# Attention values computed up front for all heads, token-major, as two units of seven products, in a hybrid attention and mLSTM kernel

## The chip, the cores and the metric

The kernel runs on one core of one Trainium2 chip. The metric is the time of one execution on the device in microseconds (us), as the median of several runs: 1439.41 us before (three runs, 1439.31 to 1439.99). Beside the times there is one profiled execution, whose span is 1437.5 us.

The core has a tensor engine (PE in the rows, TensorE in the text; PEld is its weight load), a vector engine (DVE, VectorE), a scalar engine (ACT, ScalarE), GpSimd (POOL) and SyncE (SP), which does nothing here but issue DMAs. Each engine works through its own instructions in the order in which they stand in the program, and engines wait for each other by semaphores.

## The reference

A model of two layers (h + mixer, then h + gated feed-forward, each behind a norm; a final norm) on 512 tokens of 1024 channels, in float32. The first layer's mixer is the dilated attention that the change touches (`xn` below is the normalised input), the second's an mLSTM.

```python
SEQ, D_MODEL, DEPTH = 512, 1024, 2
DIL_CONFIGS = ((128, 1), (512, 4), (2048, 16))     # window, dilation of the three groups
ATTN_HEADS, ATTN_HEAD_DIM = 8, 128
...
def dilated_attention_mixer(xn, positions, w_in, w_out):
    B, S, _ = xn.shape
    proj = (xn @ w_in).reshape(B, S, N_GROUPS, 3, ATTN_HEADS, ATTN_HEAD_DIM)
    scale = ATTN_HEAD_DIM ** -0.5
    outs = []
    lses = []
    for g, (window, dilation) in enumerate(DIL_CONFIGS):
        q = apply_partial_rope(proj[:, :, g, 0], positions) * scale
        k = apply_partial_rope(proj[:, :, g, 1], positions)
        v = proj[:, :, g, 2]
        o, lse = dilated_window_attention(q, k, v, window, dilation)
        outs.append(o)
        lses.append(lse)
    wts = jax.nn.softmax(jnp.stack(lses), axis=0)
    o = jnp.einsum('gbsh,gbshd->bshd', wts.astype(xn.dtype), jnp.stack(outs))
    return o.reshape(B, S, ATTN_WIDTH) @ w_out
```

In the attention, the projection of the normalised tokens gives queries, keys and values for three groups (g0, g1, g2: dilations 1, 4, 16) and eight heads of 128 columns. Each group's attention has its own softmax, and the groups are joined by a softmax over their log-sums. With 512 tokens g1 and g2 are four independent residues of 128 tokens each, and g0 is a band of blocks.

## The kernel before, in words

**Precision.** A float32 product is made of three fp32r matmuls, high x high, high x low and low x high (SPLITS). Every operand is therefore split in two: ScalarE copies it to fp32r (the high part, `_h`), VectorE subtracts that from the original (the low part, `_l`). For weights this is `split_chunk` (L203 to L210): a chunk is 128 x 1024 floats, 512 KB, loaded by SP in `load_chunk` (L200), high part on ScalarE (L208), low part on VectorE (L209). Three raw chunks, three high and three low parts are in flight (W_BUFS). The activations x are transposed at the start and split into eight pairs of tiles, `xa_h` and `xa_l` (`split_act`, L223 to L227), of 128 channels x 512 tokens each; the tokens stand in the order residue by residue ("token-major by residue"), so that g1 and g2 find their 128 tokens together.

**The normaliser.** x is split without its reciprocal norm r, which is applied to results. r is made by VectorE in small steps (`inverse_rms`, L307): a Newton iteration, a split of r into `xrhl`, eight diagonals `xdg` (L323), and two matmuls `xbc` (L329) that spread r over all partitions; VectorE copies this to `xrbc` (L330). `xrbc` scales queries and keys; `rtok`, r per token as a column, scales the token-major values.

**Projections.** `project` (L244) makes 256 columns (two heads of one group) of queries or keys channel-major: weights stationary, 512 tokens moving, 48 matmuls of 128x512 in two weight chunks (k0 and k1) of 24. VectorE reads out the result times `xrbc` (L724 for g0, L726 for the others), shuffles 32 partitions for the rotary embedding (L535), multiplies by the sines (L538) and adds (L541). `project_tokens_wide` (L281) makes the g1 and g2 values of a pair: 128 tokens stationary, 512 columns moving (256 of g1, 256 of g2), four chunks of 24 matmuls, rows L289 (loads) and L297 (matmuls); ScalarE copies the results with the scale r (L767).

**The attention, pair by pair.** Four pairs of heads, `a0` to `a3` (`attention_pair`, L552). For each: queries and keys of g0, g1, g2, then the values g0v (channel-major by `project`, into `vf`) and g12v. In between stand the softmax stages: `scores0` (L566, matmuls L575, masked maximum on VectorE L581, exponentials on ScalarE), `scores12` (L588, L595, L598), then `joint` (L640), which joins the groups after `exchange` (L622, a small matmul L631), `turn` (L668: eight TensorE transposes that make the g0 values token-major, in natural token order, with ScalarE copies out), `weigh` (L658) on VectorE, `transposes` (L677: 32x32 block transposes of the weights on VectorE, L681, then out to DRAM by POOL's queue, L684), `bring` (L687, back by one transfer each, L689), and `values` (L692, L699 and L704), the product with the values.

**What sets the order.** The code is written stage by stage, and `defer(n, fn)` puts a stage aside until n more weight chunks are through (`advance`, L142). RUN_AT gives these counts for scores0, scores12, the joint stage and the values, LAST_AT for scores12 and the joint stage of the last pair. So the softmax of a pair is laid between the projections of its values and of the next pair's queries and keys. `run` and `fenced` keep TensorE's order as written. SP's loads stand in the order in which chunks are asked for.

**The out-projection** takes eight heads (`oT`) split into high and low, weights `awo` in 256-column pieces c = 0 to 3. For the last pair (L804 to L813) the first weight chunk's products of c = 0 and 1 and parts of the second stand before and between that pair's two `values`.

**The start.** x arrives in four pieces; `first_mm` makes the first g0 query (`facc`) while x is still transposed; then the first g0 key (a0g0k), with `xbc` inside it; then g1's query and so on.

## Time and profile before

| | |
|---|---|
| median of three runs | 1439.41 us (1439.31 to 1439.99) |
| span of the profiled execution | 1437.5 us |
| TensorE busy | 1423.9 us (99%) |
| TensorE weight load busy | 1248.8 us (87%) |
| VectorE busy | 954.5 us (66%) |
| ScalarE busy | 605.4 us (42%) |
| GpSimd busy | 53.2 us (4%) |
| SP's and the other engines' hardware DMA queues | 131.55 MB, 29.6% of 16 DMA engines |
| DMA queue of POOL (software) | 16.30 MB, 3.7% |

The profiled execution's own time is its span of 1437.5 us, from its first to its last record; the runs, which are taken from outside, have a median 1.9 us above it. The rows of the profile give a start in us, a duration, an engine, a line (L239 is line 239 of the kernel whose profile it is), the operation, output<-inputs by the program's names, and a shape; x8 at the end: eight instructions in succession. A bracket at the end is the idle time of the engine before the row, and what released it. The 40 slices of the page each cover 36 us, and a digit is a busy share in tenths. Matmul rows start one after the other at less than their own length, since they are pipelined.

### The profile page before, as it was taken

The page shows a single profiled execution, that of the slowest core. Times are in us where ns is not written, and L with a number is a line of the kernel's source. Part 1 is how long each engine was busy: PE and PEld are TensorE (multiplying, and loading weights), DVE is VectorE, ACT ScalarE, POOL GpSimd, SP SyncE. Part 2 cuts the span into 40 slices and gives each one's busy share as a digit, 9 for nine tenths or more (in the row PEclk, how much of TensorE's full clock was granted, in tenths as well). Part 3 has the DMA queues.
Part 4 walks back from the last instruction along what each step waited for, and adds up shares of the span by engine and source line. Part 5 has one row for each costly group of instructions (what it writes and reads, how often), then busy time and mean ns, then how long its engine had stood idle before and what let it go on. Part 6 is the DMA issues. An engine that isn't in the chain of part 4 may idle for free. (4 is left out here: it accounts for less than half of the span.)

```text
span 1437.5 us, 20297 instructions
## 1 busy us (share of the span) xinstructions
PE 1423.9 (99%) x8050; PEld 1248.8 (87%) x8050; DVE 954.5 (66%) x1663; ACT 605.4 (42%) x1031; POOL 53.2 (4%) x91
## 2 busy tenths in 40 slices
PE   9999999999999999999999999999999999999998
PEld 7888888888888888999998888798888899998887
DVE  7857556557567487787782358987758777776233
ACT  5333224224225343544462233785434345455223
POOL 1001001001001000000000010100000000001001
PEclk9999999999999999999999999999999999999999
DMA  6326225234334424323233232222232333224231
GB/s 193 99 89 197 75 88 182 90 103 134 122 103 124 148 88 132 104 74 118 89 96 95 95 97 82 82 73 60 74 103 89 117 118 107 77 82 132 74 105 72
DMA packets 130903, 150.27 MB, mean 105 GB/s; under 512 B 6324, under 2 KB 120308, under 8 KB 130808
## 3 DMA queue, kind: packets, MB, share of 16 engines
q1 hardware_dynamic: 125616, 131.55, 29.6%
q0 software_dynamic: 3536, 16.30, 3.7%
q8 instruction: 63, 1.03, 0.3%
q10 hardware_dynamic: 1656, 1.12, 0.2%
q14 instruction: 32, 0.26, 0.1%
HBM read 138.99 MB, written 9.96 MB: 104 GB/s over the span
## 5 line engine op out<-in xcount | busy, mean ns | idle before, releaser
L1440 PE MATMUL fin<-fw_h,f1hh 128*128 128x512 f32 (+1 forms) x198 | 72.8, 368 | 0.0
L1440 PE MATMUL fin<-fw_l,f1hh 128*128 128x512 f32 (+1 forms) x198 | 72.6, 366 | 0.0
L1440 PE MATMUL fin<-fw_h,f1hl 128*128 128x512 f32 (+1 forms) x198 | 72.5, 366 | 0.0
L209 DVE TENSOR_TENSOR fw_l<-fw_w,fw_h 128x1024 fp32r<-128x1024 f32 x22 | 27.1, 1233 | 65.5 <-ACT fw_h L208 65.5
L239 PE MATMUL fo<-f0hh,fo_k_h 128*128 128x512 f32 x176 | 68.5, 389 | 0.0
L239 PE MATMUL fo<-f0hl,fo_k_h 128*128 128x512 f32 x176 | 68.5, 389 | 0.0
L239 PE MATMUL fo<-f0hh,fo_k_l 128*128 128x512 f32 x176 | 68.5, 389 | 0.0
L209 DVE TENSOR_TENSOR fo_k_l<-fo_k_w,fo_k_h 128x1024 fp32r<-128x1024 f32 (+1 forms) x24 | 27.2, 1134 | 62.0 <-ACT fo_k_h L208 62.0
L208 ACT ACTIVATE fo_k_h<-fo_k_w 128x1024 fp32r<-128x1024 f32 (+1 forms) x24 | 23.7, 989 | 74.7 <-PE fo L239 74.6
L208 ACT ACTIVATE fw_h<-fw_w 128x1024 fp32r<-128x1024 f32 x22 | 23.3, 1060 | 67.8 <-PE fin L1440 63.6
L1440 PEld LDWEIGHTS fin<-fw_l,f1hh 128*128 128x128 f32 x198 | 37.4, 189 | 6.0 <-DVE fw_l L209 0.2
L1440 PEld LDWEIGHTS fin<-fw_h,f1hh 128*128 128x128 f32 x198 | 37.4, 189 | 6.0
L1440 PEld LDWEIGHTS fin<-fw_h,f1hl 128*128 128x128 f32 x198 | 37.3, 189 | 6.0
L239 PEld LDWEIGHTS fo<-f0hh,fo_k_h 128*128 128x128 f32 x176 | 33.0, 188 | 6.9
L239 PEld LDWEIGHTS fo<-f0hl,fo_k_h 128*128 128x128 f32 x176 | 33.1, 188 | 6.9
L239 PEld LDWEIGHTS fo<-f0hh,fo_k_l 128*128 128x128 f32 x176 | 33.1, 188 | 6.7
L239 PE MATMUL f1j<-n_h,f1j_h 128*128 128x512 f32 x96 | 37.5, 391 | 0.0
L239 PE MATMUL f0j<-n_h,f0j_h 128*128 128x512 f32 x96 | 37.5, 391 | 0.0
L239 PE MATMUL f0j<-n_h,f0j_l 128*128 128x512 f32 x96 | 37.4, 390 | 0.0
L239 PE MATMUL f1j<-n_h,f1j_l 128*128 128x512 f32 x96 | 37.4, 390 | 0.0
L239 PE MATMUL f1j<-n_l,f1j_h 128*128 128x512 f32 x96 | 37.4, 389 | 0.0
L239 PE MATMUL f0j<-n_l,f0j_h 128*128 128x512 f32 x96 | 37.4, 389 | 0.0
(2101 smaller groups left out, 4859.7 us busy)
## 6 DMA issues: line engine op xcount, KB each, us to landing
f0j_w<-in_ffn_w_in_dram SPq DMA_DIRECT2D x28, 512.0 KB, 4.9
f1j_w<-in_ffn_w_in_dram SPq DMA_DIRECT2D x28, 512.0 KB, 3.6
fw_w<-in_ffn_w_out_dram SPq DMA_DIRECT2D x22, 512.0 KB, 3.9
fo_k_w<-in_ffn_w_out_dram SPq DMA_DIRECT2D x20, 512.0 KB, 3.5
awo_k_w<-in_attn_w_out_dram SPq DMA_DIRECT2D x8, 512.0 KB, 7.4
mv_k_w<-in_mlstm_w_in_dram SPq DMA_DIRECT2D x8, 512.0 KB, 3.6
mqk_k_w<-in_mlstm_w_in_dram SPq DMA_DIRECT2D x8, 512.0 KB, 3.7
mo_k_w<-in_mlstm_w_in_dram SPq DMA_DIRECT2D x8, 512.0 KB, 3.7
```

The lines of the kernel that those rows point to most:

```text
L208: nc.scalar.activation(hi[:, :n], raw[:, :n], AF.Copy)
L209: nc.vector.tensor_tensor(lo[:, :n], raw[:, :n], hi[:, :n].bitcast(F32), op=ALU.subtract)
L239: nc.tensor.matmul(acc, whl[a][:, k, m * P:(m + 1) * P], pairs[b][kk], start=(kk == 0 and (a, b) == SPLITS[0]), stop=(kk == nk - 1 and (a, ...
L1440: nc.tensor.matmul(acc[i][:, cs], a[a_][kk][:, tb * P:(tb + 1) * P], whl[b_][:, k, cs], start=(kk == 0 and (a_, b_) == SPLITS[0]), stop=(k ...
```

## The change

**Values.** All g0 values (1024 columns) and the g1 and g2 values of heads 0 to 3 (pairs 0 and 1; 512 columns each) are made (`values_stage`) right after the first g0 key, before the first g1 query. The g0 values form one unit `v0`, two halves of 512 columns; the g1 and g2 values of heads 0 to 3 form a second unit `v12`, whose two "halves" are g1's and g2's 512 columns. Pairs 2 and 3 make their g1 and g2 values as before. Each unit is a Strassen-Winograd scheme: the product of weights (1024 channels x 2 x 512 columns) with tokens (1024 channels x 2 x 256 tokens) as seven block products instead of eight (V_ORDER: a11, a12, s1, s2, s3, s4, a22), each of 24 matmuls with 128 tokens stationary and 512 weight columns moving, in two weight chunks of 12.

**Sums ahead.** The scheme needs sums of token blocks and of weight blocks. The tokens' forms T1 to T4 are made once, on VectorE, from a fresh copy of x times the gain (eight scalings L557, differences L561, L566, L567, L572), and split into high (ScalarE) and low (VectorE, L545 and L547); both units use them. The weight sums are made twice per unit, partly on VectorE (L637, L640), partly by loads of POOL's queue that add to what is in the tile (L604: a22 onto a21, later a21 onto a11); plain loads go by SP (L606). Results accumulate across products in PSUM (c, p, u banks), are copied out by ScalarE (L647), and two products are folded onto what was copied out, by VectorE (L650).

**Layout.** v0's results come out token-major by residue, into two staging tiles `vstage0` and `vstage1`. 32 copies of 64 KB on SP's queue (`settle`, L694) lay them out in natural order as `v0`, in the place ("heads") of the fresh copy of x. The head outputs later overwrite the g0 values head by head. `turn`, the 32 TensorE transposes and `natural_rstd` (with its small matmul) are gone. v12's results are used as they come, since g1 and g2 take tokens by residue.

**Order.** The values of pairs 0 and 1 no longer stand between the softmax stages; RUN_AT and LAST_AT are one chunk earlier for the later stages. In the out-projection three column pieces, c = 0, 1 and 2, instead of two have their first chunk ahead of the last pair's values. Some tiles of the start (angles, cosines, squares) move to other buffers.

The matmuls of the program go from 4220 to 4172 of the 128x512 form, and from 204 to 172 of the 128x128 form.

```diff
-RUN_AT = (2, 3, 5, 10)
-LAST_AT = (2, 4)
+RUN_AT = (2, 2, 4, 9)
+LAST_AT = (1, 3)
...
-        def natural_rstd():
...
-        defer(4, natural_rstd)
...
+            def scaled(ks):
+                for k in ks:
+                    nc.vector.tensor_scalar(xg[:, k], h[k], col("attn", k), None, op0=ALU.mult)
+
+            def first():
+                scaled(range(4))
+                nc.vector.tensor_tensor(z, half1(lo_), half2(lo_), op=ALU.subtract)
+                token_form("T1", z)
+
+            def second():
+                scaled(range(4, 8))
+                nc.vector.tensor_tensor(half2(lo_), half2(hi_), half2(lo_), op=ALU.subtract)
+                nc.vector.tensor_tensor(half2(hi_), half2(hi_), z, op=ALU.add)
+                token_form("T2", half2(hi_), -1.0)
+
+            def third():
+                token_form("T3", half2(lo_))
+                nc.vector.tensor_tensor(half1(hi_), half2(hi_), half1(hi_), op=ALU.subtract)
+                token_form("T4", half1(hi_))
...
+        V_ORDER = (("a11", "B11"), ("a12", "B21"), ("s1", "T1"), ("s2", "T2"), ("s3", "T3"), ("s4", "B22"), ("a22", "T4"))
+
+        class Values:
...
+            def prepare(self, n=1):
+                for _ in range(n):
+                    if not self.todo:
+                        return
+                    if not self.raw:
+                        self.begin()
+                    key, ch = self.todo.pop(0)
+                    first, own = self.raw["first", ch], self.raw["own", ch]
+                    nm = "%s%s%d" % (self.name, key, ch)
+                    if key in ("a12", "a22"):
+                        src = self.raw[key, ch] = wp.tile([P, 1024], F32, tag="wraw", name=nm + "_w", bufs=W_BUFS)
+                        self.load(key, ch, src)
+                    else:
+                        src = first if key in ("a11", "s3") else own
+                    self.made.append(split_chunk((src, 1024, lambda t: t.rearrange("p (k n) -> p k n", k=2), nm)))
+                    if key == "s1":
+                        nc.vector.tensor_tensor(own, own, first, op=ALU.add)
+                        self.load("a21", ch, first, True)
+                    elif key == "s2":
+                        nc.vector.tensor_tensor(own, own, self.raw["a12", ch], op=ALU.add)
+
+            def run(self, following, hooks={}):
...
+                    for ch in range(2):
+                        whl = self.made.pop(0)
+                        (self.prepare if self.todo else following)(1)
+                        for t in range(2):
+                            with fenced():
+                                for k in range(2):
+                                    for a, b in SPLITS:
+                                        nc.tensor.matmul(
+                                            banks[name][t], token_tile(okey, a, 2 * ch + k, t), whl[b][:, k],
+                                            start=(fresh and (ch, k) == (0, 0) and (a, b) == SPLITS[0]),
+                                            stop=((ch, k) == (1, 1) and (a, b) == SPLITS[-1]), skip_group_check=True)
...
+                        elif key == "a12":
+                            copy(dest(0, t), bk, r(t))
...
+                        elif key == "s3":
+                            fold(dest(1, 2 + t), bk, nr(2 + t))
...
+        def staged_values():
+            stage = [ap.tile([P, TB, 512], F32, tag="v12", name="vstage%d" % i, bufs=2) for i in range(2)]
+
+            def settle(i):
+                for c in range(4):
+                    for b in range(4):
+                        nc.sync.dma_start(v_all[0][32 * c:32 * c + 32, b, i * 512:(i + 1) * 512],
+                                          stage[i][32 * b:32 * b + 32, c])
+            return stage, settle
...
+        v0_unit = Values("v0", [columns(2 * D), columns(2 * D + 512)], lambda i, tb: stage[i][:, tb])
+        v12_unit = Values("v12", [columns(5 * D), columns(8 * D)], lambda i, tb: v_all[1][i][:, tb])
+        stage, settle = staged_values()
+        nrtok = ap.tile([P, TB], F32, name="nrtok")
+        nc.vector.tensor_scalar(nrtok, rtok, -1.0, None, op0=ALU.mult)
+        both(v0_unit.prepare)
+
+        def values_stage():
+            forms = token_forms()
+            v0_unit.prepare()
+            forms[0]()
+            v0_unit.run(v12_unit.prepare, {"a12": forms[1], "s1": forms[2]})
+            v_all.append(ap.tile([P, TB, D], F32, tag="heads", name="v0"))
+            for i in range(2):
+                settle(i)
+            vq = [ap.tile([P, TB, 512], F32, tag="v12", name="vq%d" % i, bufs=2) for i in range(2)]
+            v_all.append(vq[::-1])
+
+            def g1q(n):
+                ready.append(split_chunk(weight_chunk(w_in, len(ready), 3 * D, 4, "a0g1q_k%d" % len(ready))))
+            v12_unit.run(g1q)
...
-                (joint, turn, lambda: weigh(0), lambda: transposes(0), lambda: weigh(1), lambda: transposes(1),
+                (joint, lambda: weigh(0), lambda: transposes(0), lambda: weigh(1), lambda: transposes(1),
...
-            project(pair, w_in, 2 * D + pr * 256, KC, evac_f, nm + "g0v")
+            if pr < 2:
+                vt.extend(lambda c, i, g=g: v_all[1][g][:, c, (2 * pr + i) * P:(2 * pr + i + 1) * P] for g in range(2))
+                return values
...
         out_part(0, out_first, 0)
-        out_part(1, out_weights(1, 0), 0)
-        whl = [out_weights(c, 1) for c in range(2)]
+        for c in (1, 2):
+            out_part(c, out_weights(c, 0), 0)
+        whl = [out_weights(c, 1) for c in range(3)]
         for i in range(2):
             out_part(i, whl[i], 1, (0, 1))
             run(lambda: last_values(i, head_split))
-        for k in range(2, 4):
-            for c in range(2):
-                out_part(c, whl[c], 1, (k,), k == 3)
-    out_project(pair, attn_w_out[0], KC, "awo", first=2)
+        out_part(2, whl[2], 1, (0, 1))
+        for c in range(3):
+            out_part(c, whl[c], 1, (2, 3), True)
+    out_project(pair, attn_w_out[0], KC, "awo", first=3)
```

Three places show how the instructions stand. The first is VectorE around the rotary work of the first g0 query and key (a0g0q, a0g0k; `rot` is the rotary's shuffled half). Before, it is followed by the read-out of the g1 query:

```order
L535 STREAM_SHUFFLE rot_379<-a0g0k_1_381 32x512
L538 TENSOR_TENSOR rot_377<-rot_377,sinr_112 32x1024
L538 TENSOR_TENSOR rot_379<-rot_379,sinr_112 32x1024
L541 TENSOR_TENSOR a0g0_q_376<-a0g0_q_376,rot_377 32x512 x2
L541 TENSOR_TENSOR a0g0_k_378<-a0g0_k_378,rot_379 32x512 x2
L726 TENSOR_TENSOR a0g1_q_450<-a0g1q_0_452,xrbc_331 128x512
L535 STREAM_SHUFFLE rot_451<-a0g1q_0_452 32x512
```

With the change (vz is the token difference for T1, v0a121 the second chunk of the block a12 of unit v0, xg the copy of x, v0s10 and v0s11 the two chunks of s1):

```order
L524 TENSOR_TENSOR rot_378<-rot_378,sinr_111 32x1024
L524 TENSOR_TENSOR rot_380<-rot_380,sinr_111 32x1024
L527 TENSOR_TENSOR a0g0_q_377<-a0g0_q_377,rot_378 32x512 x2
L527 TENSOR_TENSOR a0g0_k_379<-a0g0_k_379,rot_380 32x512 x2
L561 TENSOR_TENSOR vz_452<-xg_451 128x1024
L210 TENSOR_TENSOR v0a121_l_488<-v0a121_w_485,v0a121_h_487 128x1024
L566 TENSOR_TENSOR xg_451<-xg_451 128x4x256
L545 TENSOR_TENSOR vT1_462<-vz_452,vT1_462 128x1024
L567 TENSOR_TENSOR xg_451<-xg_451,vz_452 128x4x256
L210 TENSOR_TENSOR v0s10_l_517<-v0own0_358,v0s10_h_516 128x1024
L210 TENSOR_TENSOR v0s11_l_535<-v0own1_359,v0s11_h_534 128x1024
L547 SCALAR_TENSOR_TENSOR vT2_513<-xg_451,vT2_513 128x1024
```

The g1 query's read-out has moved behind both units; the rotary work is followed by the sums and splits of unit v0.

The second place is SP's queue between the first keys and the values. Before, it holds weight loads alone:

```order
L200 DMA a0g1k_k_w<-in_attn_w_in_dram 128x4x256 x2
L200 DMA a0g2q_k_w<-in_attn_w_in_dram 128x4x256 x2
L200 DMA a0g2k_k_w<-in_attn_w_in_dram 128x4x256 x2
L200 DMA a0g0v_k_w<-in_attn_w_in_dram 128x4x256 x2
L289 DMA a0g12v_k_w<-in_attn_w_in_dram 128x2x256 x8
```

With the change (v0 is the natural-order tile of the g0 values, v12own, v12a12 and v12a22 the weights of the second unit):

```order
L606 DMA v12own1_709<-in_attn_w_in_dram 128x2x512
L694 DMA v0_750<-vstage0_352 32x512
L694 DMA v0_750<-vstage1_353 32x512 x5
L694 DMA v0_750<-vstage0_352 32x512 x8
L694 DMA v0_750<-vstage1_353 32x512 x11
L606 DMA v12a120_w_787<-in_attn_w_in_dram 128x2x512
L606 DMA v12a121_w_805<-in_attn_w_in_dram 128x2x512
L606 DMA v12a220_w_971<-in_attn_w_in_dram 128x2x512
L606 DMA v12a221_w_989<-in_attn_w_in_dram 128x2x512
L201 DMA a0g1q_k0_w_1009<-in_attn_w_in_dram 128x4x256
```

The settling copies stand between the first weights of v12 and its later ones.

The third place is VectorE behind the joint stage of pair 0 (a0pB is the block-transposed weights of a0; a1g1k_k1_l the low part of the second chunk of a1's g1 key). Before:

```order
L681 STREAM_TRANSPOSE a0pB_1032<-a0p0_374 128x15x4x32
L663 TENSOR_SCALAR a0p1_375<-a0p1_375,a0cf_995 128x256 x3
L666 TENSOR_SCALAR a0p1_375<-a0p1_375,a0cf_995 128x2x128 x4
L209 TENSOR_TENSOR a1g0k_k0_l_1178<-a1g0k_k0_w_1175,a1g0k_k0_h_1177 128x1024
L681 STREAM_TRANSPOSE a0pB_1047<-a0p1_375 128x15x4x32
L209 TENSOR_TENSOR a1g0k_k1_l_1208<-a1g0k_k1_w_1205,a1g0k_k1_h_1207 128x1024
L724 TENSOR_TENSOR a1g0_q_1100<-a1g0q_0_1102,xrbc_331 128x512
```

With the change:

```order
L846 STREAM_TRANSPOSE a0pB_1595<-a0p1_376 128x15x4x32
L521 STREAM_SHUFFLE rot_1610<-a1g1q_0_1611 32x512
L890 TENSOR_TENSOR a1g1_q_1609<-a1g1q_1_1612,xrbc_321 128x512
L521 STREAM_SHUFFLE rot_1610<-a1g1q_1_1612 32x512
L755 ISA a1p0_1353,a1own_1351<-a1s0_1677,acst_109 128x128
L755 ISA a1own_1351 128x1
L755 ISA a1p0_1353,a1own_1351<-a1s0_1677,acst_109 128x256
...
L524 TENSOR_TENSOR rot_1610<-rot_1610,sinr_111 32x1024
L781 TENSOR_SCALAR a1nb_1349<-a1own_1351 128x4
L210 TENSOR_TENSOR a1g1k_k1_l_1746<-a1g1k_k1_w_1743,a1g1k_k1_h_1745 128x1024
```

The joint stage of a0 has moved from beside a1's g0 query and key to beside a1's g1 query and key, and the first half of a1's score passes (L755) now stands between the transposes and that split.

## The prediction

> **What bounds the kernel now.** I read the page's busy shares first, then the windows of the attention stage, then the timelines of TensorE and VectorE at the places that the change touches.

> ```profile
> PE 1423.9 (99%) x8050; PEld 1248.8 (87%) x8050; DVE 954.5 (66%) x1663; ACT 605.4 (42%) x1031; POOL 53.2 (4%) x91
> DVE  7857556557567487787782358987758777776233
> ```
> ```profile
> 28.00:32.00 4.00, 3.71 (x17) 2.75 (x16) 3.96 (x15) 1.06 (x1) 0.00 (x0) 1.00 0.00 1
> 32.00:36.00 4.00, 4.00 (x20) 3.29 (x19) 4.00 (x9) 0.99 (x1) 0.00 (x0) 1.00 0.56 165
> 36.00:40.00 4.00, 4.00 (x19) 3.33 (x18) 4.00 (x8) 0.08 (x1) 0.00 (x0) 1.00 0.28 97
> 40.00:44.00 4.00, 4.00 (x19) 3.31 (x18) 4.00 (x7) 1.07 (x1) 0.00 (x0) 1.00 0.01 2
> 119.40:231.90 112.50, 112.50 (x552) 95.25 (x551) 68.70 (x156) 36.09 (x83) 5.53 (x10) 1.00 0.39 120
> ```

> TensorE is busy for 1423.9 of 1437.5 us, so a matmul taken out is time gained, as long as its operands are there. The columns of a windows row are the length, then the busy time of PE, weight load, DVE, ACT, POOL, then clock and DMA. VectorE works 68.7 us in a pair's 112.5 us, but from 28 to 44 us, where the new value units are to run, it has no gap at all: it holds the rotary work of the first query and key.

> **What goes.** Four rows of TensorE's timeline give the pace (start, length, operation):

> ```profile
> 444.99 1.04 PE L305 MATMUL a3vT<-cst,a3vf 128*128 128x128 f32 x8
> 445.78 0.48 PE L297 MATMUL a3g12v<-a3g12v_k_h,xa_h 128*128 128x512 f32 x1
> ...
> 446.56 0.40 PE L297 MATMUL a3g12v<-a3g12v_k_h,xa_h 128*128 128x512 f32 x1
> ...
> 456.56 0.39 PE L297 MATMUL a3g12v<-a3g12v_k_h,xa_l 128*128 128x512 f32 x1
> ...
> 471.79 1.83 PE L699 MATMUL a3o<-a3pT,a3v 128*128 128x128 f32 x14 [1.24 <-DMA a3pT<-a3pD]
> ```

> From 446.56 to 456.56 there are 44 steps of the form that the units use (tokens stationary, 512 weight columns moving), 0.2273 us each. The units hold 2 x 7 products of 24 such matmuls, 336, for the 384 of the g0 values and of pairs 0 and 1: 48 fewer, **10.9 us**. Eight value transposes take 445.78 - 444.99 = 0.79 us of TensorE per pair. In the last pair TensorE already waits 1.24 us for the weights of the values (471.79), and a shorter way there only lengthens that wait, so three pairs count: **2.4 us**. The one small matmul of the reciprocal norm is 0.1. In the last pair 108 matmuls lie between the exchange and the first value product, before and after (48 and 60; 24 and 84), so the new out-projection order is worth nothing. Removed ACT work (transposed copies) hides behind TensorE. Sum: **-13.4 us**. If each transposing pair counted, it would be -14.2.

> **What comes: unit v0 against VectorE's queue.** VectorE takes its instructions in order. These are its rows from the norm on, and the TensorE rows beside them:

> ```profile
> 28.44 1.65 DVE L323 TENSOR_SCALAR xdg<-cst,xrhl 128x128 fp32r<-128x128 f32 x8
> ...
> 31.14 0.68 DVE L330 COPY xrbc<-xbc 128x512 f32<-128x512 f32 x1
> ...
> 32.94 1.20 DVE L209 TENSOR_TENSOR a0g1q_k_l<-a0g1q_k_w,a0g1q_k_h 128x1024 fp32r<-128x1024 f32 x1
> 34.07 0.67 DVE L724 TENSOR_TENSOR a0g_q<-a0g0q,xrbc 128x512 f32<-128x512 f32 x1
> ...
> 38.98 2.33 DVE L538 TENSOR_TENSOR rot<-rot,sinr 32x1024 f32<-32x1024 f32 x2
> ...
> 42.45 1.28 DVE L541 TENSOR_TENSOR a0g_k<-a0g_k,rot 32x512 f32<-32x512 f32 x2
> 43.66 0.67 DVE L726 TENSOR_TENSOR a0g_q<-a0g1q,xrbc 128x512 f32<-128x512 f32 x1
> ```
> ```profile
> 23.10 0.39 PE L239 MATMUL a0g0k<-xa_h,a0g0k_k_h 128*128 128x512 f32 x1
> ...
> 29.45 0.47 PE L329 MATMUL xbc<-xdg,ones_r 128*128 128x512 f32 x1 [0.29 <-DVE xdg L323]
> ```
> ```profile
> L1143 DVE TENSOR_SCALAR conv<-pre,cols 128x512 f32<-128x512 f32 x8 | 4.0, 502 | 0.1
> L977 DVE TENSOR_TENSOR f0j6S<-f0j_w,f0j6A x1: 1215/1215/1215, 556.8 to 556.8; 128x1024 f32<-128x1024 f32 x1
> L208 ACT ACTIVATE a0g1q_k_h<-a0g1q_k_w x2: 1058/1060/1061, 25.6 to 28.5; 128x1024 fp32r<-128x1024 f32 x2
> ```

> A 1024-column pass in a row of such costs 32.94 to 34.07, 1.13 us; the plain sum of two chunks (L977) has the same length as a split. I take 1.14 for every split, sum and token-form pass. The eight scalings of x (0.50 each, the row of conv has that shape) now stand among the small steps of the norm, ahead of the diagonals xdg that end at 28.44 + 1.65 = 30.1 today. Of their 4.0 some 0.4 fill gaps between those steps, so the diagonals end at 33.7 and the first four, which the first xbc needs, at 32.9. TensorE comes to the first xbc 42 matmuls into the key projection, at 23.10 + 42 x 0.2273 = 32.6, and three matmuls later to the second: a wait of some 0.3, which is what xbc waits today (0.29). Bounds 0 and 1. Entry: 0.

> After the diagonals VectorE does one more split (to 34.8), and from xrbc on the rows stand as today: 31.14 to 43.66 is 12.5 us with one split in it. Behind them come the difference for T1 (1.14) and the split of a12's second chunk (1.14): 14.8 us, so that split ends at 49.6. TensorE has until then the end of the key projection (4), a11 (24) and the first half of a12 with single matmuls of the second half: it stands at its 43rd matmul after the second xbc (33.9), 43 x 0.2273 + 0.2 later, at 43.9. **Wait: 5.7 us.** This is a difference of two runs of rows from one common point, and a later xbc shifts both.

> From the split's end X on, everything is in passes of 1.14. The split of s1 is the fourth pass (X + 4.6); TensorE has 12 matmuls (2.7): wait **1.8**. The split of s2 is the eleventh (T1, T2, T3 low parts, three sums for x, two splits, two weight sums before it): X + 12.5; TensorE has 24 matmuls (5.5) after s1 began, X + 10.0: wait **2.5**. The split of s3 is the sixteenth, X + 18.2; TensorE at X + 17.7: **0.5**. From s4 on VectorE is ahead. Passes that read what the pass before wrote cannot overlap it by the 0.08 us between 1.21 and 1.13; some three do: 0.3. Unit v0: **+10.8 us**. Bounds: with 1.05 for a pass 9.0, with 1.21 for each 12.5.

> The loads are in time: the accumulating load that s3 needs goes out when the weight sums are done (X + 9.1) and has until X + 16; the nearest POOL loads are these.

> ```profile
> a0pD<-a0pB POOLq DMA_DIRECT2D x8, 240.0 KB, 4.9
> a0pT<-a0pD POOLq DMA_DIRECT2D x2, 960.0 KB, 8.3
> ```

> 512 KB lies between 4.9 and 8.3. At 8.3 for the second, X + 18, the wait of 0.5 grows to 2; I take 6 and no more wait.

> **What comes: the settling copies on SP's queue.** The second chunk pair of v12 (a12) is loaded by SP after all 32 copies that lay v0's rows out anew, and the last 11 of those need the unit's last ACT copies.

> ```profile
> 8.10 0.43 SPq L404 DMA_DIRECT2D cst<-in_shape_constants_dram  x1
> ```
> ```profile
> a0g1k_k_w<-in_attn_w_in_dram SPq DMA_DIRECT2D x2, 512.0 KB, 3.5
> L767 ACT ACTIVATE a1v<-a1g12v,xr x4: 686/687/688, 228.7 to 232.1; 128x512 f32<-128x512 f32 x4
> ```

> With E the end of v0's matmuls: ACT's second copy ends at E + 0.9 (0.69 and two handovers); seven copies are then still to be issued, at 0.40 (the 64 KB load of SP took 0.43): E + 3.8; the load lands 3.5 later, E + 7.3; ACT split 1.06 and VectorE split 1.21: E + 9.6. TensorE has a11 and two matmuls of a12, 26 steps, E + 5.9. **+3.6 us.** Bounds: 0.2 per copy and a load of 3.4 give 2.1; 0.6 and 4.9 (another median of such loads) give 6.5. Everything on SP behind them, the loads of g1q, has the whole unit as cover.

> **What is pressed together: pairs 0 and 1.** Without value matmuls, a pair's softmax runs beside the next pair's projections. VectorE keeps 68.7 less six splits (6.8) = 62 us, TensorE 112.5 less 144 x 0.2273 and 0.8, 79 us. On the whole that fits; the tight place is the second chunk of a1g1k, whose split now stands behind the exchange, both transposes and the first half of a1's scores.

> ```profile
> 98.36 3.73 PE L595 MATMUL a0s<-a0g_k,a0g_q 128*128 128x128 f32 x32
> 101.85 0.48 PE L297 MATMUL a0g12v<-a0g12v_k_h,xa_h 128*128 128x512 f32 x1
> ...
> 158.79 3.20 PE L575 MATMUL a1s<-a1g_k,a1g_q 128*128 128x128 f32 x16
> 161.64 0.58 PE L239 MATMUL a1g1k<-xa_h,a1g1k_k_h 128*128 128x512 f32 x1
> ```
> ```profile
> 113.27 0.29 DVE L633 TENSOR_TENSOR a0ex<-a0xps,cst 128x128 f32<-128x128 f32 x1 [2.84 <-PE a0xps L631]
> ...
> 119.12 2.17 DVE L681 STREAM_TRANSPOSE a0pB<-a0p 128x1920 f32<-128x1920 f32 x1
> ...
> 124.15 2.16 DVE L681 STREAM_TRANSPOSE a0pB<-a0p 128x1920 f32<-128x1920 f32 x1
> ```
> ```profile
> L581 DVE CUSTOM_DVE_ANT_0 a1p<-a1s,acst 128x256 f32<-128x256 f32 x6 | 2.2, 412 | 0.0
> ```

> From the exchange on VectorE needs: to the first transpose 5.85, and the rotation of a1g0k in between (1.13 + 1.2, of which 0.5 fills gaps); to the second 5.03 less a split that stands elsewhere, 3.9, and a read-out 0.6; the transpose 2.1; two shuffles and a read-out (from 34.07 to 38.98, four of each take 4.91) 1.9; four score passes 1.3; rotation and split 2.3. Sum 19.8, and it starts 1.4 late, since the last read-out and shuffle of a1g0k come first: 21.2. TensorE needs 0.2, 48 matmuls (10.9), the scores 161.64 - 158.79 = 2.85, 24 matmuls and 6 that need the high parts alone (6.8): 20.8. **+0.4 us** per pair, twice: **+0.9**. Bounds 0 and 3 each: two sums of 20 us against each other. The transposed weights for the values come back later by about the same 1.5 as TensorE does, so no wait there; in pairs 2 and 3 the value matmuls give the old cover.

> **Sum.** -13.4 + 10.8 + 3.6 + 0.9 = +1.9 us on the profiled span of 1437.5 us, which lies 1.9 us under the median of 1439.4 us: 1439.4 us span, **1441.3 us** as a run. A measurement of this kernel can tell about 0.2% (2.9 us), so this is no change by that bound, at its slower edge.

> **Rivals.** *A, faster:* only the first wait is real. While TensorE waits 5.7 us for a12, VectorE draws ahead, and if the passes for s1 and s2 overlap better than rows of 1.13 say, 1.8 + 2.5 + 0.5 + 0.3 go: 1436; with the copies on SP hidden too, 1433. For it: VectorE's slice there is a mean of 7 to 8 tenths. Against: windows of 4.00 in 4.00, and the passes run from SBUF at the same 1.13 everywhere.

> *B, slower:* VectorE binds in pairs 0 and 1 as well, and SP is slower. Place: the a1g1k and a2g1k splits, 3 us each instead of 0.4, and 6.5 for the copies: 1441.3 + 5.2 + 2.9 = 1449. It decides from the point where the chain from the exchange exceeds 20.8 us. For it: 21.2 against 20.8 leaves no room, and an exponential or DMA that comes late adds at once. Against: the same chain with slack today in pairs 0 to 2.

> *C, slower:* after a long wait matmuls run at half pace.

> ```profile
> 1.52 4.59 PE L107 MATMUL idle<-idle_w,ones_r 128*128 128x512 f32 x10 [1.52 <-DVE idle_w L102]
> ```

> The first ten of the kernel took 4.59 us, 0.46 each, twice 0.2273. Such a restart costs 2.3 us. Before s1 some 1.8 of it are hidden by the wait, behind the copies none: 0.5 + 2.3, and as much again if the 2.5 before s2 counts: 1444 to 1446. Against: nothing between 6 and 1430 us shows it, as no wait there is over 2 us. [...] The granted clock in the rows above reads 1.00 throughout, so no run here shows it yet.

> **How the numbers follow.** Forecast 0.45, with its own range 1438 to 1445; A 0.17; B 0.24; C 0.14. Without the forecast's spread the others reach from 1433 to 1449 and a little beyond by their own doubts: range 1434 to 1451. Faster by over 0.2% (under 1436.5): A, 0.17. Slower (over 1442.3): B, C, and a sixth of the forecast, 0.45. The same: 0.38.

> **What will show it.** VectorE full from 30 to about 68 us, TensorE waiting 5 to 6 us for the low part of a12's second chunk or for T1's high part, then 1 to 3 us before s1 and s2; a wait of 3 to 4 us in v12 at a12, ended by a load; matmul rows at 0.227 after each wait (C: 0.45); a wait before the second chunk of a1g1k and a2g1k of under 1 us (B: 3). It is wrong if these waits together lie under 10 us, or if one stands at a place not named here.

## The result

With the change the kernel takes 1449.66 us (median of four runs, 1448.54 to 1450.94) against 1439.7 us before on the same chip (1439.31 to 1440.89): a ratio of 1.0071, with a 95% interval of 1.0057 to 1.0086. It is 10 us slower. The profiled execution has a span of 1447.7 us, 10.2 us longer than that of before.

The page of the changed kernel, busy shares and slices:

```profile
PE 1417.3 (98%) x7968; PEld 1238.4 (86%) x7968; DVE 991.4 (68%) x1705; ACT 617.0 (43%) x1019; POOL 63.7 (4%) x99
```

The page's rows for two engines and the granted clock, in slices of 36 us:

```profile
PE   9779999999999999999999999999999999999998
DVE  7945687775767387777782358987758777877233
PEclk9989999999999999999999999999999999999999
```

TensorE has less to do, 1417.3 us for 1423.9, and it is no longer full in the second and third slice; there the granted clock also leaves its nine in one place. The waits of TensorE (what it waited for: us in total, times, longest) name the places:

```profile
PE v_acc L665 <- ACT v12a_h L209: 7.8, 1, 7.8
PE v_o L665 <- DVE v0s_l L210: 2.7, 1, 2.7
PE v_s L665 <- ACT vT L543: 2.5, 1, 2.5
PE a3o L863 <- DMA a3pT<-a3pD: 2.2, 1, 2.2
```

The longest waits are for the high part of a12 in the second unit, for the low part of s2 and the high part of T1 in the first, and, ahead of these, 1.77 us for the copy `v_o` that starts the third pair of accumulators. The wait for the last pair's weights, `a3o`, grew from 1.24 to 2.2 us.

Where the 10.2 us come from is read from the starts of three groups, by tile, before (first two rows) and with the change:

```profile
L239 PE MATMUL a0g1q<-xa_h,a0g1q_k_h x16: 388/389/390, 35.0 to 45.2; 128*128 128x512 f32 x16
L239 PE MATMUL f0j<-n_h,f0j_h x96: 388/389/486, 508.6 to 574.7; 128*128 128x512 f32 x96
```
```profile
L240 PE MATMUL a0g1q<-xa_h,a0g1q_k_h x16: 389/389/389, 134.1 to 144.3; 128*128 128x512 f32 x16
L240 PE MATMUL f0j<-n_h,f0j_h x96: 389/389/486, 518.0 to 584.0; 128*128 128x512 f32 x96
```

From the first g1 query to the feed-forward block (f0j) the kernel took 508.6 - 35.0 = 473.6 us, and now takes 383.9: 89.7 less. The 384 matmuls that left this stretch are 87.3 us, the 32 transposes of all four pairs 3.2, and the longer wait of the last pair takes 1.0 back; that leaves 0.2 unexplained. The units themselves run from 34.17 (next rows) to 134.1, 99.9 us, where 336 matmuls at 0.2273 would be 76.4: **23.5 us too long**. The start is 0.9 earlier (in the other kernels that start like this one, e1, e2, e3, e5, e8, e9 and e10, the units begin at 34.30 to 35.05, so this 0.9 is hardly a gain of the change), and everything behind the attention 0.8 longer. -89.7 + 99.9 - 0.9 + 0.8 = +10.1.

Within the units, TensorE's timeline (start, length, operation; in brackets the wait ahead of it):

```profile
34.17 0.39 PE L665 MATMUL v_acc<-v0a_h,xa_h 128*128 128x512 f32 x1
...
38.89 0.50 PE L665 MATMUL v_acc<-v0a_h,xa_h 128*128 128x512 f32 x1 [1.77 <-ACT v_o L674]
...
48.76 0.50 PE L665 MATMUL v_s<-v0s_h,vT 128*128 128x512 f32 x1 [2.48 <-ACT vT L543]
...
50.68 0.63 PE L665 MATMUL v_acc<-v0a_h,xa_l 128*128 128x512 f32 x1
51.10 0.63 PE L665 MATMUL v_acc<-v0a_l,xa_h 128*128 128x512 f32 x1
...
52.98 0.39 PE L665 MATMUL v_s<-v0s_h,vT 128*128 128x512 f32 x1
...
61.80 0.50 PE L665 MATMUL v_o<-v0s_l,vT 128*128 128x512 f32 x1 [2.65 <-DVE v0s_l L210]
...
66.71 0.40 PE L665 MATMUL v_o<-v0s_l,vT 128*128 128x512 f32 x1
...
84.94 0.39 PE L665 MATMUL v_acc<-v12a_h,xa_h 128*128 128x512 f32 x1
...
98.36 1.22 PE L665 MATMUL v_acc<-v12a_h,xa_h 128*128 128x512 f32 x2 [7.83 <-ACT v12a_h L209]
...
101.07 0.63 PE L665 MATMUL v_acc<-v12a_l,xa_h 128*128 128x512 f32 x1
101.50 0.63 PE L665 MATMUL v_acc<-v12a_h,xa_l 128*128 128x512 f32 x1
...
103.97 0.40 PE L665 MATMUL v_acc<-v12a_h,xa_h 128*128 128x512 f32 x1
...
106.73 0.39 PE L665 MATMUL v_s<-v12s_h,vT 128*128 128x512 f32 x1
```

Two things are to be seen. Unit v0 lasts from 34.17 to 84.94, 12.6 us more than its 168 matmuls; unit v12 is 11.0 us too long, 7.83 of it in one wait. And behind three of the waits the matmuls stand 0.425 us apart (50.68 to 51.10, 101.07 to 101.50) instead of 0.227. From 48.76 to 52.98 eleven matmuls take 4.22 us, 1.7 more than eleven steps; from 61.80 to 66.71 fourteen take 1.7 more; from 98.36 to 103.97 twelve take 2.9 more. So the 23.5 us are 15.3 of waits (7.4 in v0, 7.8 in v12), 6.3 of half pace, and 1.9 that is left: at the waits (1.77, 0.21, 0.33, 2.48, 2.65, 7.83) the matmul ahead ends 0.16 to 0.27 us after the next one would have started, and the wait is counted from there; the first step behind a wait is some 0.1 longer than the others; and a transpose of gains (0.23) stands in v0. That is about 1.5 of the 1.9.

Why the load of a12 was late stands in SP's queue:

```profile
84.75 8.19 SPq L694 DMA_DIRECT2D v<-vstage  x13
92.99 1.62 SPq L606 DMA_DIRECT2D v12a_w<-in_attn_w_in_dram  x3
```
```profile
85.14 0.69 ACT L647 ACTIVATE vstage<-v_o,nrtok 128x512 f32<-128x512 f32 x1 [0.67 <-PE v_o L665]
...
97.26 1.06 ACT L209 ACTIVATE v12a_h<-v12a_w 128x1024 fp32r<-128x1024 f32 x1 [6.04 <-DMA v12a_w<-in_attn_w_in_dram]
```

ScalarE's last copy into the staging tile ends at 85.83. Eleven settling copies then still stand ahead of a12's load; they take until 92.99, 0.6 us each. The load lands at 97.2, 4.2 later.

### The profile page after: what moved, and what is told of

The parts are those of the page before. It is cut to its first block, busy times and chain, and to the rows that moved or that the text cites. A ratio compares the mean times of both kernels' runs of the same rounds, so it can differ in the third digit from the quotient of the medians.

```text
span 1447.7 us, 20235 instructions
## 1 busy us (share of the span) xinstructions
PE 1417.3 (98%) x7968; PEld 1238.4 (86%) x7968; DVE 991.4 (68%) x1705; ACT 617.0 (43%) x1019; POOL 63.7 (4%) x99
## 5 line engine op out<-in xcount | busy, mean ns | idle before, releaser
L209 ACT ACTIVATE fo_k_h<-fo_k_w 128x1024 fp32r<-128x1024 f32 (+1 forms) x24 | 23.7, 989 | 74.7 <-PE fo L240 74.7
L209 ACT ACTIVATE fw_h<-fw_w 128x1024 fp32r<-128x1024 f32 x22 | 23.3, 1060 | 67.8 <-PE fin L1604 67.8
## 6 DMA issues: line engine op xcount, KB each, us to landing
f0j_w<-in_ffn_w_in_dram SPq DMA_DIRECT2D x28, 512.0 KB, 5.0
f1j_w<-in_ffn_w_in_dram SPq DMA_DIRECT2D x28, 512.0 KB, 3.5
fw_w<-in_ffn_w_out_dram SPq DMA_DIRECT2D x22, 512.0 KB, 3.8
fo_k_w<-in_ffn_w_out_dram SPq DMA_DIRECT2D x20, 512.0 KB, 3.5
awo_k_w<-in_attn_w_out_dram SPq DMA_DIRECT2D x8, 512.0 KB, 3.7
mv_k_w<-in_mlstm_w_in_dram SPq DMA_DIRECT2D x8, 512.0 KB, 3.7
mqk_k_w<-in_mlstm_w_in_dram SPq DMA_DIRECT2D x8, 512.0 KB, 3.7
mo_k_w<-in_mlstm_w_in_dram SPq DMA_DIRECT2D x8, 512.0 KB, 3.6
```

Of the source, the lines that this page charges most:

```text
L209: nc.scalar.activation(hi[:, :n], raw[:, :n], AF.Copy)
```

## The experiments

The theory after the result: the settling copies ahead of a12's loads on SP's queue cost v12 its 11 us; VectorE's queue costs v0 its waits; the half pace is a consequence of the waits. The rivals: late buffers or loads, weights that come late in the slow stretches, and sums that stall TensorE wherever they are made. All times are medians beside runs of the kernel before on the same chip (1438.9 to 1439.7).

| kernel | against the change | us | ratio to before, 95% interval |
|---|---|---|---|
| the change | | 1449.66 | 1.0071 (1.0057 to 1.0086) |
| e1 | copies behind the loads of a12 | 1439.66 | 1.0003 (0.9994 to 1.0012) |
| e2 | rotary work later | 1434.29 | 0.9963 (0.9949 to 0.9978) |
| e3 | the wait filled with matmuls | 1449.38 | 1.0069 (1.0054 to 1.0084) |
| e5 | out-projection order | 1447.5 | 1.0053 (1.0038 to 1.0068) |
| e6 | eight plain products in both units | 1436.41 | 0.998 (0.9971 to 0.9989) |
| e9 | accumulator banks exchanged | 1449.56 | 1.0069 (1.0053 to 1.0084) |
| e8 | e2, e5 and e9 together | 1432.51 | 0.9953 (0.994 to 0.9965) |
| e10 | e2 and e5 together | 1432.54 | 0.9955 (0.9942 to 0.9967) |
| e11 | v0 plain, v12 seven products, e5 | 1433.84 | 0.9962 (0.9948 to 0.9975) |
| e12 | e11 with the scalings later | 1431.32 | 0.9949 (0.9936 to 0.9963) |

### e1: the settling copies behind the loads

```diff
-            for i in range(2):
-                settle(i)
-            vq = [ap.tile([P, TB, 512], F32, tag="v12", name="vq%d" % i, bufs=2) for i in range(2)]
-            v_all.append(vq[::-1])
+            def settled():
+                for i in range(2):
+                    settle(i)
+                vq = [ap.tile([P, TB, 512], F32, tag="v12", name="vq%d" % i, bufs=2) for i in range(2)]
+                v_all.append(vq[::-1])
...
-            v12_unit.run(g1q)
+            v12_unit.run(g1q, {"a12": settled})
```

> One thing is changed against the change: the 32 settling copies are asked for after the loads of a12 of unit v12, no longer before them; which matmuls, splits and sums are made stays as it is. Theory (the 7.83 us wait before a12 of v12 and the half clock behind it, 2.7 us, both come from the eleven copies of 0.61 us each that stand ahead of the load on SP's queue): the wait goes below 1 us, the rows behind it stand 0.227 apart, and the time falls by about 10.5 us to 1439. Rival (the load would be as late without the copies, because its raw buffer comes free late or ScalarE and VectorE are late): a wait of 4 us or more stays there and the time is 1446 or more.

SP's queue and TensorE's waits of this kernel:

```profile
76.94 0.37 SPq L606 DMA_DIRECT2D v12a_w<-in_attn_w_in_dram  x1
77.36 19.61 SPq L694 DMA_DIRECT2D v<-vstage  x26
```
```profile
49.64 0.50 PE L665 MATMUL v_s<-v0s_h,vT 128*128 128x512 f32 x1 [2.51 <-ACT vT L543]
...
54.23 0.50 PE L665 MATMUL v_s<-v0s_l,vT 128*128 128x512 f32 x1 [1.56 <-DVE v0s_l L210]
...
62.18 0.80 PE L665 MATMUL v_o<-v0s_l,vT 128*128 128x512 f32 x1 [2.17 <-DVE v0s_l L210]
```

The loads of a12 leave by 76.94, ahead of 26 copies, and the 7.8 us wait is gone; the waits of v0 stay. The time falls by 10.0 us, as the theory gave (10.5), to that of the kernel before. Unit v12 lasts 39.6 us, 9.6 less than with the change: that is what the copies cost, the wait and the half pace behind it. The other 1.4 of its 11.0 stay, 1.06 of them a wait for ScalarE's copy `vq`.

These rows show one thing more. Here no half pace follows the wait of 2.51 us, but a wait of 1.56 us comes up at the second chunk of s1, and from s1's start to s2's this kernel needs 62.18 - 49.64 = 12.5 us where the change needs 61.80 - 48.76 = 13.0. So of the 1.7 us that the change loses there at half pace, all but 0.5 would otherwise have been a wait for VectorE.

### e2: the rotary work of the first query and key later

```diff
-            v0_unit.run(v12_unit.prepare, {"a12": forms[1], "s1": forms[2]})
+            v0_unit.run(v12_unit.prepare, {"a12": forms[1], "s1": forms[2], "s3": rotations, "s4": forms[3]})
...
-                        if pr == 0 and g == 0:
-                            rotate(qk[0], sh0, True)
...
-                    values_stage()
+                    values_stage(lambda: (rotate(qk[0], sh0, True), rotate(qk[1], sh1, True)))
```

(`forms[3]` is the T4 part of `third`.)

> Against the change only the place of the first query's and key's rotary products and sums on VectorE (4.7 us) is changed: behind the weight sums, with the low part of T4 after them. Theory (VectorE's queue sets the waits of unit v0): the splits of s1 and s2 come some 3.5 to 4.7 us earlier, and so do s2 and all behind it; the time falls by about 4 us to 1445.5, the waits before s1 and s2 do not vanish, since what stands behind them is passes of VectorE alone. Rival (the waits of v0 come from loads or from ScalarE): the time stays within 1 us of the change's 1449.7.

It fell by 15.4 us, four times the 4 expected. SP's queue shows why:

```profile
74.93 1.50 SPq L608 DMA_DIRECT2D v12a_w<-in_attn_w_in_dram  x2
77.23 26.44 SPq L696 DMA_DIRECT2D v<-vstage  x32
```

The order that the scheduler makes of the changed program has the copies behind a12's loads here too, so this kernel holds e1's edit as well; so do e8 and e10. The rotary's own part is e2 against e1: 1439.66 - 1434.29 = 5.4 us by the medians. In the two profiled executions both units together take 85.4 us for 89.8, 4.5 less, within the 3.5 to 4.7 of VectorE's time that was moved. So VectorE's queue does set v0's waits. With the copies ahead of the loads the move was not measured by itself.

### e3: the wait filled with matmuls

```diff
+            def fill():
+                bank = ps.tile([P, 512], F32, tag="t", name="fill", bufs=1)
+                for _ in range(34):
+                    nc.tensor.matmul(bank, ones_r, pair[0][0], start=True, stop=True)
+            v12_unit.run(g1q, {"a12": lambda: behind(fill)})
```

> Against the change TensorE is given 34 additional matmuls of 128x512 into a bank that nobody reads, right ahead of a12 of unit v12, where it waits 7.83 us; they take 7.7 us at full rate. Theory C (matmuls run at half rate because TensorE has just stood still): the 13 matmuls behind the wait stand 0.227 apart instead of 0.425, the granted clock reads 1.00 there, and the time falls by 2.7 us to 1447. Rival (they are slow because their weights come late, or because of the DMA traffic of that moment): the 13 matmuls stay at 0.425 and the time at 1449.7.

```profile
91.67 8.10 PE L725 MATMUL fill<-xa_h,ones_r 128*128 128x512 f32 x34
...
100.65 0.73 PE L665 MATMUL v_acc<-v12a_h,xa_h 128*128 128x512 f32 x2 [0.54 <-ACT v12a_h L209]
...
102.48 0.40 PE L665 MATMUL v_acc<-v12a_h,xa_h 128*128 128x512 f32 x1
102.72 0.40 PE L665 MATMUL v_acc<-v12a_l,xa_h 128*128 128x512 f32 x1
...
107.06 0.39 PE L665 MATMUL v_s<-v12s_h,vT 128*128 128x512 f32 x1
```

The matmuls behind the filled wait keep their full pace (102.48 to 102.72; the granted clock from 100 to 107 us is 1.00), though their weights come from the same late load. a12 takes 107.06 - 100.65 = 6.4 us instead of 106.73 - 98.36 = 8.4. So the half pace comes from TensorE having stood still, not from late weights. The time itself did not fall by the 2.7 expected (0.3, inside the intervals): in this build the load is late by more, a12 starts 2.3 us later than with the change (unit v12 itself 1.3 later, the rest in the copies), so the 2.0 gained are spent ahead of it.

### e5: the out-projection's order

```diff
-        for i in range(2):
-            out_part(i, whl[i], 1, (0, 1))
-            run(lambda: last_values(i, head_split))
-        out_part(2, whl[2], 1, (0, 1))
-        for c in range(3):
-            out_part(c, whl[c], 1, (2, 3), True)
+        out_part(0, whl[0], 1, (0, 1))
+        out_part(1, whl[1], 1, (0, 1))
+        run(lambda: last_values(0, head_split))
+        out_part(2, whl[2], 1, (0, 1))
+        run(lambda: last_values(1, head_split))
+        for k in (2, 3):
+            for c in range(3):
+                out_part(c, whl[c], 1, (k,), k == 3)
```

> Against the change only the order of the out-projection's matmuls around the last pair's values is changed: the second-chunk products of column pieces 0 and 1 both ahead of the first values, those of piece 2 between the two values, then heads 6 and 7 one after the other over the three pieces. Theory (the last pair's values wait 2.2 us for their transposed weights, since they come 12 matmuls sooner after them than before the change): 12 matmuls (2.7 us) more ahead of them fill the wait, 1447.5. Rival (the wait moves to the splits of heads 6 and 7, which then have less cover): the time stays at 1449.7.

1447.5, as expected: the 2.2 us wait for the last pair's weights is gone from the list of waits, and no other took its place. The reason given for the wait is not right, though: 108 matmuls lie between the exchange and the first value product before and with the change. What is gone from there is the last pair's transposes, 0.8 us. Nor is the wait the same in every kernel with the change's order: 1.0 to 1.2 us in e1, e2 and e9, 1.8 in e3, 2.8 in e6.

### e6: eight plain products

Both units by `project_tokens_wide`, without token forms, weight sums and adding loads; copies and tiles as in the change.

```diff
-            v0_unit.run(v12_unit.prepare, {"a12": forms[1], "s1": forms[2]})
+            plain("v0", v0_unit.parts, v0_unit.dest)
...
-            v12_unit.run(g1q)
+            plain("v12", v12_unit.parts, v12_unit.dest)
```

> Against the change both units are computed as eight plain products (per 512 columns four weight chunks of 24 matmuls, as pairs 2 and 3 still do) at the same place and into the same tiles; token forms, weight sums and adding loads are gone, 48 matmuls (10.9 us) come back; the settling copies stand where the change has them. Theory (VectorE's sums and forms cost unit v0 its 7.4 us of waits and 3.2 us of half clock): these go, so the time is about that of the change, 1449.7 within 1.5. Rival (the waits of v0 come from elsewhere, read-outs or loads, and stay): 1457 or more.

Three windows over the units (length; busy PE, PEld, DVE, ACT, POOL; clock, DMA share, GB/s), of the change and then of the plain kernel:

```profile
30.00:60.00 30.00, 24.34 (x94) 17.59 (x92) 29.59 (x47) 12.34 (x15) 2.26 (x2) 0.94 0.23 52
60.00:90.00 30.00, 28.20 (x117) 23.11 (x118) 18.74 (x19) 13.22 (x15) 2.51 (x3) 0.94 0.81 178
90.00:120.00 30.00, 22.14 (x85) 17.20 (x84) 14.94 (x13) 13.80 (x16) 2.39 (x2) 0.83 0.55 137
```
```profile
30.00:60.00 30.00, 29.75 (x132) 24.35 (x131) 19.90 (x36) 7.97 (x10) 0.00 (x0) 1.00 0.37 105
60.00:90.00 30.00, 30.00 (x134) 24.84 (x133) 6.37 (x6) 7.95 (x9) 0.00 (x0) 1.00 0.49 136
```

Without forms and sums VectorE drops from 29.59 to 19.90 and TensorE has no wait in the units. The time is 1436.41, 13 us under the expectation, and for a reason that the expectation had left out: it kept the copies' price, but the plain kernel's copies go in two halves of 16, from 54.0 to 64.2 us and from 75.8 to 86.7, with loads behind each, and the chunks already loaded cover them: no wait of TensorE shows there, though the profiled execution was the longest of ten (1439.15). So v0's 12.6 us belong to the seven products (sums and forms on a full VectorE), and v12's 11.0, by e1 9.6 of them, to the copies as they fell there. Values up front without the seven products, with all else of the change, make the kernel 3.0 us faster than before (2.5 were forecast for transposes and norm).

### e9 and e8: other accumulator banks

e9 exchanges the banks of the second and third pairs of accumulators, so that ScalarE's copy behind a11 need not wait for VectorE's reading of the first query. The values of e9 and e8 differ; probably the third accumulators then do not take up the copied a11 sums everywhere. The instructions are the same, and the times are read as usual.

```diff
-                        banks[name] = bank(*{"c": ("acc", 3), "p": ("s", 2)}[name])
+                        banks[name] = bank(*{"c": ("acc", 3), "p": ("o", 2)}[name])
...
-                                banks["u"] = bank("o", 2)
+                                banks["u"] = bank("s", 2)
```

> Against the change only the accumulator banks of unit v0 and v12 are exchanged (third pair of accumulators in the free banks), so that the copy behind a11 need not wait for VectorE's read-out of the first query. Theory (VectorE's queue decides further on): the 1.77 us wait goes and the next two grow by as much, 1449.7 within 0.7. Rival (each wait counts by itself): 1447.7.

1449.56: no gain. The 1.77 us wait is gone, but TensorE now waits 1.3 us for the reading of the first key and 1.0 for the copies: the waits ahead of s1's 2.5 add up to 2.3 us in both kernels. The theory had the lost time come back before s1 and s2; it came back one step earlier, behind the next reading in VectorE's queue. The copies' 7.6 stay. The edit thus moved a wait and removed none.

> The rotary work later and the new out-projection order together, and the copy that starts the third pair of accumulators goes to the two banks that are free instead of the two that hold the first query's product until VectorE has read it. Theory (VectorE's queue sets when the split of s2 is there, whatever TensorE does before it): the bank's 1.7 us wait goes but reappears before s2; only the last pair's wait of 1.0 is gained over the rotary kernel's 1434.3: 1433.3. Rival (each wait of TensorE counts by itself): 1431.5 or less. By either it stays under the kernel before, 1439.6.

1432.51, between VectorE's queue (1433.3) and its rival (1431.5): this run does not decide between them.

### e10: rotary work and out-projection order

> The rotary work later and the new out-projection order together, with the accumulator banks of the change. Theory (VectorE's queue decides before s2): the same time as with the exchanged banks, 1432.5, or up to 0.8 more; the last pair's wait of 1.0 us for its weights is gone, two waits of together 2.4 us stay before s2 and s3 of unit v0. Rival (each wait counts by itself): 1.7 us more than with the exchanged banks, 1434.2.

1432.54, the same as with the exchanged banks, where the rival had 1434.2. The 1.75 us wait for the bank stands again in this kernel, but the waits ahead of s1 add up to 2.9 us with either choice of banks: the exchange only put another reading in VectorE's queue in its place. That fits the theory. A kernel in which such a wait goes and none takes its place was not run.

### e11 and e12: one unit plain, the other with seven products

```diff
+            plain(0)
+            for form in forms:
+                form()
             v_all.append(ap.tile([P, TB, D], F32, tag="heads", name="v0"))
+            settle(0)
+            plain(1)
+            v12_unit.prepare(2)
...
+            v12_unit.run(g1q, {"a12": settled})
```

(`settled` copies the second half; the out-projection is e5's. In e12 `form()` becomes `behind(form, engine=DVE)`.)

> The g0 values as eight plain products, their first half's settling copies between the halves and the second's after the loads of a12; VectorE makes the token forms beside them; then v12 as seven products as in the change; out-projection in the new order. Theory (the seven products pay where VectorE is ahead of TensorE, and only there): no wait over 0.5 us in either unit, 24 matmuls (5.45 us) fewer than the plain kernel's 1436.4, and its last pair's wait of 2.2 to 2.8 us filled: 1428.7. Rival (the forms and sums stall TensorE wherever they are made): waits of 4 us or more in one of the units, 1433 or more.

Neither unit has a wait over 0.5 us, as the theory has it, but the time is 1433.84, not 1428.7. TensorE's timeline names the rest, a wait of 3.07 us for the norm's diagonals and some 1.6 us of half pace behind it:

```profile
37.11 0.47 PE L331 MATMUL xbc<-xdg,ones_r 128*128 128x512 f32 x1 [3.07 <-DVE xdg L325]
...
38.41 0.63 PE L298 MATMUL v<-v_k_l,xa_h 128*128 128x512 f32 x1
38.84 0.63 PE L298 MATMUL v<-v_k_h,xa_l 128*128 128x512 f32 x1
```

> As the kernel with one unit, but the eight scalings for the token forms stand behind the rotary work of the first query and key on VectorE instead of among the small steps of the norm. Theory (the 3.1 us wait for the diagonals there came from the scalings, and the half clock of some 1.8 us behind it came from the wait): both go, no wait over 0.5 us in the units, 1429. Rival (the small steps are late for another reason, or the forms are now late for the seven products): a wait of 2 us or more stays, 1432 or more.

```profile
31.82 0.47 PE L331 MATMUL xbc<-xdg,ones_r 128*128 128x512 f32 x1 [1.76 <-DVE xdg L325]
```
```profile
28.59 1.23 DVE L210 TENSOR_TENSOR v_k_l<-v_k_w,v_k_h 128x1024 fp32r<-128x1024 f32 x1 [1.50 <-ACT v_k_h L209]
```
```profile
90.00:120.00 30.00, 30.00 (x133) 24.74 (x132) 19.22 (x19) 16.23 (x19) 2.39 (x2) 1.00 0.53 133
```

1431.32, 2.5 us better, and the half pace is gone, but 1.76 of the 3.07 us stay. In e11 two weight splits stood among the norm's small steps beside the scalings, each behind a wait of 1.4 us for ScalarE's high part; in e12 one of them still does (28.59). The scalings were one cause of the late diagonals, not the only one. From 60 to 120 us TensorE is full, the seven products of v12 among them. This kernel beats before by 7.7 us (0.9949), with half of the change's products saved.

## Why the prediction came out as it did

The forecast was 1441.3, the time 1449.7. It lies in the range given (1434 to 1451) and on the side with the largest chance, but outside the forecast's own range (1438 to 1445).

- **What goes, -13.4:** right. Matmuls and transposes left as counted; four pairs' transposes count (3.2), and the last pair's longer wait takes 1.0 of it back, which is 2.2 net for the 2.4 forecast. That the out-projection's order is worth nothing was right of the forecast's step; that another order is worth 2.2 was not seen.
- **Entry, 0:** 0.9 better than that. The diagonals were ready when TensorE came, so the first xbc does not wait at all (0.3); 0.5 more is that the first query's matmuls begin earlier (8.24 for 8.73), which in e1 and e10 they do not (9.28, 9.25).
- **Unit v0, +10.8:** 12.6. VectorE's queue was forecast well. These are two of its rows:

```profile
47.55 1.21 DVE L210 TENSOR_TENSOR v0a_l<-v0a_w,v0a_h 128x1024 fp32r<-128x1024 f32 x1
...
60.53 2.35 DVE L210 TENSOR_TENSOR v0s_l<-v0own,v0s_h 128x1024 fp32r<-128x1024 f32 x2
```

  a12's second chunk was split at 48.8 (forecast 49.6), the first chunk of s2 at 61.7 (62.1). One sum of this step is off: 24 matmuls from X + 12.5 on end at X + 18.0, not X + 17.7, so the wait before s3 is 0.2 by its own rows, not 0.5; none showed there. The places were partly wrong: the step had TensorE waiting 5.7 in one piece at a12, but 1.77 of it came ahead of a12, behind the copy `v_o`, whose bank VectorE had yet to read. The step did not look at which bank that copy writes. The waits add up to 7.4; the half pace behind two of them adds 3.4, which the step priced at nothing and gave to rival C.
- **Settling copies, +3.6:** 11.0 (8.1 without the half pace), the largest miss, above the bounds (2.1 to 6.5). The step took seven copies of 0.40, from one 64 KB load; there were eleven of 0.6, and the load took 4.2 for 3.5. The half pace, 2.9, comes on top.
- **Pairs 0 and 1, +0.9:** no wait. The window from 150 to 340 us shows TensorE full (the 150 to 230 us of it: 80.00 of 80.00). With this rival B's place falls too: its 1449 is close to the time, but its splits cost nothing, and only its dearer copies were real.

```profile
150.00:230.00 80.00, 80.00 (x374) 66.81 (x373) 62.23 (x145) 25.11 (x67) 5.55 (x10) 1.00 0.36 107
```

- **Rival C** (0.14) was real: 6.3 us at half pace, and e3 shows where it comes from (the granted clock from 98 to 106 us is 1.00 with the wait filled, 0.63 with the change). As C said, the part before s1 is mostly hidden: e1 shows that 1.2 of it would have been a wait otherwise. It had been weighed down because no wait of before is over 2 us. The miss of 8.3 us (10.2 for 1.9) is C's 6.3 and 4.5 for the number and length of the copies, less 1.6 for v0's waits, 0.9 for the pairs and 0.9 for the entry, and 0.9 in what is left.
- **Rival A** fell: the passes did not overlap better (from 48.8 to 61.7 us VectorE needed 12.9 for the 12.5 forecast).

By the signs that the prediction itself named, it was wrong in part. A wait stands at a place that it did not name (1.77 us ahead of a12), the wait in v12 is 7.8 us for 3 to 4, and behind three waits the matmuls stand 0.425 us apart. That the time still lies in the range is partly luck: v0's waits, the pairs and the entry came out 3.4 us better than priced and made up for a part of what the half pace and the copies cost.

## What to carry to other kernels

Matmuls taken out are worth their time only where the operands of the rest are made in time: the seven products saved 10.9 us of TensorE and paid for it on an engine that had no gap at that place, while the same products one unit later showed no wait (e12). Where a change puts many small transfers on a queue, count those that can leave only after the last result (here eleven, 0.6 us each), and look which load stands behind them. And add to a wait of TensorE what the matmuls behind it lose (here 1.7 us each behind 2.48 and 2.65, 2.9 behind 7.83).

## What the runs showed of the hardware

The half pace came behind waits as short as 2.48 and 2.65 us, and it did not begin and end with them. Windows of 1 us of the changed kernel (the clock is the third number from the end):

```profile
49.00:50.00 1.00, 1.00 (x4) 0.75 (x4) 1.00 (x2) 0.00 (x0) 0.00 (x0) 0.62 0.00 0
...
52.00:53.00 1.00, 1.00 (x5) 0.80 (x3) 1.00 (x2) 0.03 (x1) 0.00 (x0) 0.67 0.00 0
...
93.00:94.00 1.00, 0.00 (x0) 0.00 (x0) 0.00 (x0) 0.00 (x0) 0.00 (x0) 0.81 0.50 119
...
103.00:104.00 1.00, 1.00 (x4) 0.77 (x4) 0.31 (x1) 0.00 (x0) 0.15 (x1) 0.57 0.00 0
```

A wait of 2.48 us was enough for the fall at 49.24. It lay wholly in one step of the grid (45.83 to 49.24). In e1 a wait of 2.51 us passed without a fall (clock 1.00 from 30 to 60 us). That kernel's clock falls at 62.18, where the matmul behind the wait of 2.17 us lasts 0.80 us instead of 0.50 (0.89 from 60 to 75 us). If its grid has the same step, one step ends four times 3.41 earlier, at 48.53, and the wait, from 47.13 to 49.64, lies 1.40 us in one step and 1.11 in the next. So, as an estimate from these two waits, a wait's price depends on where in the grid it lies.

Laid out so from 10 to 120 us in the seven kernels whose clock falls there (the change, e1, e2, e3, e5, e9, e11), each step at full clock with 1.85 us or more of idle TensorE was followed by a fall, and none with 1.70 or less. In between there were both: 1.74 us in e2 and 1.76 in e5 fell, 1.77 in the change and in e3 did not. In these runs the border thus lies between 1.70 and 1.85 us, and a wait of some 1.75 us or more could cost 1.7 us on top (behind the 2.48 and the 2.65), a long one more (2.9 behind the 7.83).

The other surprise is that moving VectorE's work by some rows changed SP's order by 32 transfers (e2), through the scheduler: an experiment that moves one thing has to be read in every queue.
